# Four weight chunks to a group, and the low parts of the weights at another place in SBUF

## The chip, the cores and the metric

The kernel runs on one core of a Trainium2 chip. The metric is device time in microseconds (us): how long one execution takes. Matmuls run on TensorE (PE; PEld is its weight load), element-wise work on VectorE (DVE), ScalarE (ACT) and GpSimd (POOL), and the weights come by DMAs that SyncE (SP) issues.

## The reference

A two-layer decoder trunk over 256 tokens with 2048 features, all in float32. Layer 0 mixes tokens by a spatial gate beside a four-head attention into 256 memory tokens; layer 1 does it by a twelve-head latent attention beside the same memory attention. Each layer ends in a gated feed-forward network with a short convolution. Nearly all the work lies in the products with the weight matrices:

```python
D_MODEL, SEQ, D_FF = 2048, 256, 5632
def conv_ffn(h, w_up, cw, cb, w_down):
    a = h @ w_up                                   # 2048 x 11264
    ap = jnp.pad(a, ((0, 0), (CONV_W - 1, 0), (0, 0)))
    c = sum(ap[:, k:k + S] * cw[k] for k in range(CONV_W)) + cb
    gate, val = c[..., :D_FF], c[..., D_FF:]
    return (jax.nn.silu(gate) * val) @ w_down      # 5632 x 2048
...
for l in range(DEPTH):                             # DEPTH = 2
    ...
    x = x + jnp.concatenate([main, mo], axis=-1) @ w_out[l]
    x = x + conv_ffn(rmsnorm(x, g_ffn[l]), w_ffn_up[l], conv_w[l], conv_b[l], w_ffn_down[l])
return rmsnorm(x, g_final)
```

## The kernel before

**Three products for one.** The kernel multiplies in the type fp32r and cuts each operand in two: a high part, the copy in fp32r, and a low part, what that copy leaves of the float32 value. A product of weights W and activations X is then W_hi X_hi + W_hi X_lo + W_lo X_hi.

**Most products hold the weights still** (`gemm_fm` and `mm_fm`). An activation tile such as `xhl`, `h`, `mainhl`, `memhl`, `qhl` or `chl` has 512 columns for a block of 128 features: 256 high ones, then 256 low ones. For each 128x128 block of weights there is one **high product** (line L158): the block of `whi` is loaded into the array and all 512 columns stream past it; and one **low product** (L162): the block of `wlo` is loaded and only the 256 high columns stream. In the last layers the roles are turned round (`gemm_tm`, lines L213 to L215): blocks of activations are loaded, and `whi` and `wlo` stream; at the very end a few of these have only 256 columns.

**Chunks.** A weight chunk is 512 KB, 128 partitions by 1024 floats: two blocks of 128 rows by 512 columns, so 8 high and 8 low products. `chunk` takes a buffer `raw` (4 of them), issues the DMA into it on SP (L107), lets ACT round it into `whi` (4 buffers, L117; with a gain L122), and lets DVE write the rest, raw minus high, into `wlo` (4 buffers, L118; with a gain L123).

**Groups.** `gemm_fm` takes the chunks of a product two at a time (`together = 2`), so 16 high products stand in a row and then 16 low ones. Every second group is turned (low ones first), so that two runs of a kind meet: in the steady state 32 high, 32 low, 32 high and so on, the last run of a product and the first run of the next included. A product over 2048 features has 8 chunks, so four groups before. The very first product (`raw` is given) takes one chunk at a time, and `queries` and `keys` in layer 1 have groups of their own.

**Hooks.** Other work of the PE (transposes, attention scores and the like) is handed to `gemm_fm` as `hooks`, a table from the number of a chunk to functions. They are called after the group that holds the chunk. In layer 1 the last two heads go through the output projection `w_out` in this way: `turn` transposes their softmax (L970) and `attend` multiplies it with the values (L979, L980).

**Order.** A scheduler with its own estimates of times orders each engine's instructions, except in a few stretches that are written out by hand.

**Places.** In the built program `raw`, `whi`, `wlo` and all the activation tiles named above begin at byte 96 modulo 256 of a partition. `low_tile` gives `wlo` 64 spare floats; where it holds still, its data begin 16 floats further on, so at 160 modulo 256. Where `wlo` streams (`moves`), its data begin at 96. Every block in a tile begins at a multiple of 512 bytes from there.

Of the kernel before, what the change touches and what calls it, by code (L numbers as in the profile page):

```python
# [9 lines left out]
F32R = mybir.dt.float32r  # L10
# [6 lines left out]
P = 128  # L17
# [52 lines left out]
class Kernel:  # L70
# [20 lines left out]


    def low_tile(self, moves=False):
        w = self.wp.tile([P, 1088], F32R, tag="wlo", name=self.uid("wlo"), bufs=4)
        return w[:, :1024] if moves else w[:, 16 : 16 + 1024]


    def chunk(self, src, nk, ncol, gains=None, heads=None, raw=None, moves=False):
# [51 lines left out]

    def mm_fm(self, jobs, turn):
        mm = self.nc.tensor.matmul

        def high(js):
            for acc, wh, wl, x, first, last in js:
                mm(acc[:, :], wh, x, start=first, stop=last)  # L158

        def low(js):  # L160
            for acc, wh, wl, x, first, last in js:
                mm(acc[:, S:], wl, x[:, :S], start=False, stop=False)  # L162

        starts, ends = any(j[4] for j in jobs), any(j[5] for j in jobs)
        if ends and (starts or not turn):
            high([j for j in jobs if not j[5]])
            low(jobs)
            high([j for j in jobs if j[5]])
        elif turn and not starts:
            low(jobs)  # L170
            high(jobs)
        else:
            high(jobs)
            low(jobs)


    def gemm_fm(self, src, kbs, nblk, rhs, evict, nk=2, gain=None, hooks={}, raw=None):
        accs = [self.psum() for _ in range(nblk)]
        together = 1 if raw is not None else 2
        chunks = list(range(0, len(kbs), nk))  # L180
        groups = [chunks[i : i + together] for i in range(0, len(chunks), together)]

        def split(group):
            jobs = []
            for c in group:
                g = None if gain is None else [gain(kbs[c + i]) for i in range(nk)]
                hi, lo = self.chunk(src(kbs[c], nk), nk, nblk * P, g, raw=raw if c == 0 else None)
                for b in range(nblk):
                    cols = slice(b * P, (b + 1) * P)
                    for i in range(nk):  # L190
                        kk = c + i
                        jobs.append((accs[b], hi[:, i, cols], lo[:, i, cols], rhs(kbs[kk]), kk == 0, kk == len(kbs) - 1))
            return jobs

        ready = []
        for n, group in enumerate(groups):
            ahead = groups[n : n + 2] if raw is not None else [group]
            for g in ahead[len(ready) :]:
                ready.append(split(g))
                for f in hooks.get(-1, ()) if g is groups[0] else ():  # L200
                    f()
            self.mm_fm(ready.pop(0), n % 2 if raw is None else 0)
            for c in group:
                for f in hooks.get(c // nk, ()):
                    f()
        for b in range(nblk):
            evict(b, accs[b])

# [162 lines left out]
    def gain(self, name, k, n=1):  # L371
        c = self.g[name] + k
        return self.gT[:, c : c + n]
# [434 lines left out]
    def layer_b(self):  # L808
# [3 lines left out]
        w, wkv = t["w_in_b"][0], t["w_kv_a"]  # L812
# [5 lines left out]
        with tc.tile_pool(name="lb", bufs=1) as lb:  # L818
# [71 lines left out]
            hooks = {6: [rotate_key], 4: [lambda: fq(qhl, QR, "g_q_lat")]}  # L890
# [75 lines left out]
            def turn(h):  # L966
                p = pa.pop(h)
                acc = self.psum()
                for i in range(3):
                    nc.tensor.transpose(acc[:, i * P : (i + 1) * P], p[:, i * P : (i + 1) * P], self.ident)  # L970
                pT = self.tmp(lp, [P, 512], "pT", 3)
                nc.scalar.activation(pT[:, : 3 * P], acc[:, : 3 * P], AF.Copy)
                pa[h] = pT

            def attend(h):
                pT = pa.pop(h)
                o = self.psum()
                cols = slice(h * P, (h + 1) * P)
                mm(o[:, :S], v[:, 0, cols], pT[:, :S], start=True, stop=False)  # L979
                mm(o[:, P:S], v[:, 1, cols], pT[:, S : S + P], start=False, stop=True)  # L980
                self.split(hl[:, h, :], o[:, :S])
# [11 lines left out]
            n = GH // 2  # L993
# [27 lines left out]
            for h in (2 * n - 4, 2 * n - 3):  # L1021
                attend(h)
            ends = (2 * n - 2, 2 * n - 1)
            hooks = {2: [lambda h=h: turn(h) for h in ends], 3: [lambda h=h: attend(h) for h in ends]}
            self.w_out(1, hl, [12, 13, 14, 15] + list(range(12)), hooks, ctx.close)

    def run(self):
# [96 lines left out]
```

## Time and profile before

| What | Value |
|---|---|
| median of three runs | 2093.12 us (2093.07 to 2093.68) |
| the profiled execution | 2094.34 us, of which 2092.6 us are the span from the first to the last instruction |
| busy in the span | PE 2082.2 us, PEld 1821.7, DVE 1458.7, ACT 1139.0, POOL 398.9 |
| granted TensorE clock | 0.999 of full speed |
| read from HBM | 387.88 MB |

An entry "line engine op out<-in xcount | busy, mean" of the groups gives how many instructions of a kind there were and how long one took on average. Matmuls are pipelined, so their durations overlap; what a matmul adds to the time is the distance between two starts, which the timeline and the chain of waits give.

### The profile page before, as it was taken

How to read it: one execution, taken by the hardware profiler on the slowest of the kernel's cores; microseconds unless marked ns; L12 is line 12 of the kernel's file. 1: busy time of each engine (PE TensorE's matmuls, PEld its weight loads, DVE VectorE, ACT ScalarE, POOL GpSimd, SP SyncE). 2: the span in 40 equal slices, each digit the busy share in tenths (PEclk: the TensorE clock that was granted, in tenths of full speed). 3: DMA queues.
4: the chain of work that ended last, by engine and by line, in shares of the span. 5: the costliest groups of instructions: out<-in, count | busy, mean ns of one | idle time of the engine just before them, and what ended most of it. 6: DMA issues, size and time to landing. Idle time of an engine off the chain costs nothing.

```text
span 2092.6 us, 31012 instructions
## 1 busy us (share of the span) xinstructions
PE 2082.2 (100%) x11614; PEld 1821.7 (87%) x11614; DVE 1458.7 (70%) x2150; ACT 1139.0 (54%) x1747; POOL 398.9 (19%) x387
## 2 busy tenths in 40 slices
PE   9999999999999999999999999999999999999998
PEld 8888888888888888888888888888888888888886
DVE  6755767777756777567798875777765677746775
ACT  6754654555535655445655664456553565535554
POOL 0100133312101211012244121421210122201220
PEclk9999999999999999999999999999999999999999
DMA  8665555656556565556555534555655556555554
GB/s 272 197 216 159 161 195 188 191 188 195 191 192 191 181 201 188 194 185 190 190 192 182 176 106 159 185 190 181 192 194 194 186 188 194 196 196 189 184 191 152
DMA packets 208092, 392.01 MB, mean 187 GB/s; under 512 B 14334, under 2 KB 23876, under 8 KB 207812
## 3 DMA queue, kind: packets, MB, share of 16 engines
q1 hardware_dynamic: 207364, 388.98, 57.3%
q8 instruction: 91, 1.49, 0.3%
q10 hardware_dynamic: 576, 1.05, 0.2%
q14 instruction: 61, 0.50, 0.1%
HBM read 387.88 MB, written 2.10 MB: 186 GB/s over the span
## 4 chain that ended last, share of the span: by engine, by line
PE 99%; DMA 0%; ACT 0%; DVE 0%; issue 0%; ACTq 0%
PE ps L158 51%; PE ps L162 26%; PE ps L215 6%; PE ps L213 6%; PE ps L214 6%; PE ps L949 0%; PE ps L947 0%; PE ps L575 0%; PE ps L610 0%; DMA raw<-in_w_mem_kv 0%; PE ps L432 0%; PE ps L979 0%; PE ps L760 0%; PE ps L872 0%; PE ps L970 0%; PE ps L1051 0%
## 5 line engine op out<-in xcount | busy, mean ns | idle before, releaser
L118 DVE TENSOR_TENSOR wlo<-raw,whi 128x1024 fp32r<-128x1024 f32 x660 | 842.5, 1286 | 468.1 <-ACT whi L117 346.0
L117 ACT ACTIVATE whi<-raw 128x1024 fp32r<-128x1024 f32 x660 | 695.6, 1058 | 692.3 <-PE ps L158 511.3
L158 PE MATMUL ps<-xhl,whi 128*128 128x512 f32 x3264 | 765.0, 390 | 0.0
L158 PEld LDWEIGHTS ps<-xhl,whi 128*128 128x128 f32 x3264 | 605.1, 188 | 121.2
L662 POOL TENSOR_TENSOR a<-js,rbc 128x256 f32<-128x256 f32 x176 | 232.1, 1331 | 1094.1 <-DVE js L264 998.5
L162 PEld LDWEIGHTS ps<-xhl,wlo 128*128 128x128 f32 x3264 | 400.8, 189 | 8.4
L162 PE MATMUL ps<-xhl,wlo 128*128 128x256 f32 x3264 | 404.8, 281 | 0.0
L158 PE MATMUL ps<-h,whi 128*128 128x512 f32 x704 | 164.7, 390 | 0.0
L665 ACT ACTIVATE c<-a,cT 128x256 f32<-128x256 f32 x176 | 105.2, 598 | 98.6 <-POOL a L662 97.0
L158 PEld LDWEIGHTS ps<-h,whi 128*128 128x128 f32 x704 | 130.5, 188 | 26.0
L214 PE MATMUL ps<-wlo,h 128*128 128x512 f32 x354 | 137.1, 388 | 0.0
L213 PE MATMUL ps<-whi,h 128*128 128x512 f32 x354 | 137.0, 388 | 0.0
L215 PE MATMUL ps<-whi,h 128*128 128x512 f32 x354 | 136.6, 388 | 0.0
L158 PE MATMUL ps<-mainhl,whi 128*128 128x512 f32 x512 | 120.1, 390 | 0.0
L158 PEld LDWEIGHTS ps<-mainhl,whi 128*128 128x128 f32 x512 | 94.8, 188 | 18.9
L667 DVE SCALAR_TENSOR_TENSOR c<-a,cT,c 128x254 f32<-128x254 f32 x176 | 101.0, 586 | 0.0
L666 DVE SCALAR_TENSOR_TENSOR c<-a,cT,c 128x255 f32<-128x255 f32 x176 | 91.7, 540 | 12.9 <-ACT c L665 12.7
L123 DVE SCALAR_TENSOR_TENSOR wlo<-raw,gT,whi 128x512 fp32r<-128x512 f32 x112 | 87.1, 819 | 19.3 <-ACT whi L122 17.5
L122 ACT ACTIVATE whi<-raw,gT 128x512 fp32r<-128x512 f32 x112 | 74.7, 723 | 31.6 <-PE ps L158 14.2
L264 DVE TENSOR_TENSOR js<-ps,cr 128x256 f32<-128x256 f32 x209 | 82.2, 415 | 12.4 <-POOL a L662 12.4
L262 ACT ACTIVATE cr<-ps 128x256 f32<-128x256 f32 x243 | 79.7, 374 | 15.7 <-PE ps L158 12.1
L162 PEld LDWEIGHTS ps<-h,wlo 128*128 128x128 f32 x704 | 86.5, 189 | 1.9
(259 smaller groups left out, 1859.6 us busy)
## 6 DMA issues: line engine op xcount, KB each, us to landing
raw<-in_w_ffn_up SPq DMA_DIRECT2D x352, 512.0 KB, 3.5
raw<-in_w_ffn_down SPq DMA_DIRECT2D x176, 512.0 KB, 4.3
raw<-in_w_out SPq DMA_DIRECT2D x64, 512.0 KB, 3.5
raw<-in_w_in_a SPq DMA_DIRECT2D x56, 512.0 KB, 4.0
raw<-in_w_mem_kv SPq DMA_DIRECT2D x31, 512.0 KB, 3.8
raw<-in_w_in_b SPq DMA_DIRECT2D x16, 512.0 KB, 3.5
raw<-in_w_kv_a SPq DMA_DIRECT2D x9, 512.0 KB, 4.2
raw<-in_w_uq SPq DMA_DIRECT2D x12, 384.0 KB, 3.3
```

The source lines that it names most:

```text
L117: nc.scalar.activation(hi[:, :n], raw[:, :n], AF.Copy)
L118: nc.vector.tensor_tensor(lo[:, :n], raw[:, :n], hi[:, :n].bitcast(F32), ALU.subtract)
L123: nc.vector.scalar_tensor_tensor(lo[:, s], raw[:, s], gains[k], hi[:, s].bitcast(F32), ALU.mult, ALU.subtract)
L158: mm(acc[:, :], wh, x, start=first, stop=last)
L162: mm(acc[:, S:], wl, x[:, :S], start=False, stop=False)
L213: mm(acc, xh, wh, start=first, stop=False)
L214: mm(acc, xh, wl, start=False, stop=False)
L215: mm(acc, xl, wh, start=False, stop=last)
L662: nc.gpsimd.tensor_tensor(a, self.join(acc), rb, ALU.mult)
L665: nc.scalar.activation(c, a, AF.Identity, scale=w(2), bias=w(3))
L666: nc.vector.scalar_tensor_tensor(c[:, 1:], a[:, : S - 1], w(1), c[:, 1:], ALU.mult, ALU.add)
L667: nc.vector.scalar_tensor_tensor(c[:, 2:], a[:, : S - 2], w(0), c[:, 2:], ALU.mult, ALU.add)
```

## The change

- `gemm_fm` takes four chunks together (one, as before, in the first product). A product of 8 chunks has two groups: 32 high, 32 low, and then 32 low, 32 high; with the neighbours that makes runs of 64.
- `wlo` has six buffers instead of four. `raw` and `whi` keep four.
- `mm_fm` gets a function `between`, called between the two kinds of a group. `gemm_fm` hands it the hooks of the first half of the group's chunks; those of the second half follow the group. One hook in layer 1 gets another number (2 becomes 1).
- The data of a still `wlo` begin 19 floats on instead of 16: at 172 modulo 256 instead of 160. The activation tiles move up by 2 x 4352 bytes, which leaves them at 96 modulo 256.

```diff
     def low_tile(self, moves=False):
-        w = self.wp.tile([P, 1088], F32R, tag="wlo", name=self.uid("wlo"), bufs=4)
-        return w[:, :1024] if moves else w[:, 16 : 16 + 1024]
+        w = self.wp.tile([P, 1088], F32R, tag="wlo", name=self.uid("wlo"), bufs=6)
+        return w[:, :1024] if moves else w[:, 19 : 19 + 1024]
...
-    def mm_fm(self, jobs, turn):
+    def mm_fm(self, jobs, turn, between=lambda: None):
...
         if ends and (starts or not turn):
             high([j for j in jobs if not j[5]])
+            between()
             low(jobs)
             high([j for j in jobs if j[5]])
         elif turn and not starts:
             low(jobs)
+            between()
             high(jobs)
         else:
             high(jobs)
+            between()
             low(jobs)
...
-        together = 1 if raw is not None else 2
+        together = 1 if raw is not None else 4
...
-            self.mm_fm(ready.pop(0), n % 2 if raw is None else 0)
-            for c in group:
-                for f in hooks.get(c // nk, ()):
-                    f()
+
+            def hooked(cs):
+                for c in cs:
+                    for f in hooks.get(c // nk, ()):
+                        f()
+
+            self.mm_fm(ready.pop(0), n % 2 if raw is None else 0, lambda: hooked(group[: len(group) // 2]))
+            hooked(group[len(group) // 2 :])
...
-            hooks = {2: [lambda h=h: turn(h) for h in ends], 3: [lambda h=h: attend(h) for h in ends]}
+            hooks = {1: [lambda h=h: turn(h) for h in ends], 3: [lambda h=h: attend(h) for h in ends]}
```

What this does to the built order is shown at two places. The first is on PE, at the end of the first product of layer 1's output projection: `ps_12738` to `ps_12741` are its four sums, `ps_12969` to `ps_12972` those of the next product, `mainhl` the activations. Before:

```order
L162 MATMUL ps_12740<-mainhl_11640,wlo_12898 128x256 x2
L162 MATMUL ps_12741<-mainhl_11640,wlo_12898 128x256 x2
L158 MATMUL ps_12969<-mainhl_11640,whi_12974 128x512
L162 MATMUL ps_12738<-mainhl_11640,wlo_12904 128x256
L162 MATMUL ps_12739<-mainhl_11640,wlo_12904 128x256
L162 MATMUL ps_12740<-mainhl_11640,wlo_12904 128x256
L162 MATMUL ps_12741<-mainhl_11640,wlo_12904 128x256
L158 MATMUL ps_12969<-mainhl_11640,whi_12974 128x512
L158 MATMUL ps_12970<-mainhl_11640,whi_12974 128x512
L162 MATMUL ps_12738<-mainhl_11640,wlo_12904 128x256
```

After, at the same place:

```order
L162 MATMUL ps_12740<-mainhl_11640,wlo_12872 128x256 x2
L162 MATMUL ps_12741<-mainhl_11640,wlo_12872 128x256 x2
L158 MATMUL ps_12738<-mainhl_11640,whi_12853 128x512 x2
L158 MATMUL ps_12739<-mainhl_11640,whi_12853 128x512 x2
L158 MATMUL ps_12740<-mainhl_11640,whi_12853 128x512 x2
```

The high products of the next product no longer stand between the low ones. Over the whole program a high product follows a low one directly at 170 places before and at 92 after; a low one follows a high one at 176 and at 99.

The second is on DVE, in the feed-forward network of layer 0, where one product has just ended and its sums `ps_7356` to `ps_7359` go through the convolution (`js`, `c`, `hv`) while the low parts of the next weights are written. Before:

```order
L118 TENSOR_TENSOR wlo_7643<-raw_7641,whi_7642 128x1024
L264 TENSOR_TENSOR js_7539<-ps_7356,cr_7537 128x256
L264 TENSOR_TENSOR js_7553<-ps_7357,cr_7551 128x256
L118 TENSOR_TENSOR wlo_7649<-raw_7647,whi_7648 128x1024
L264 TENSOR_TENSOR js_7567<-ps_7358,cr_7565 128x256
L264 TENSOR_TENSOR js_7581<-ps_7359,cr_7579 128x256
L666 SCALAR_TENSOR_TENSOR c_7542<-a_7536,cT,c_7542 128x255
L666 SCALAR_TENSOR_TENSOR c_7556<-a_7550,cT,c_7556 128x255
L667 SCALAR_TENSOR_TENSOR c_7542<-a_7536,cT,c_7542 128x254
L118 TENSOR_TENSOR wlo_7687<-raw_7685,whi_7686 128x1024
```

After:

```order
L118 TENSOR_TENSOR wlo_7611<-raw_7609,whi_7610 128x1024
L271 TENSOR_TENSOR js_7539<-ps_7356,cr_7537 128x256
L271 TENSOR_TENSOR js_7553<-ps_7357,cr_7551 128x256
L118 TENSOR_TENSOR wlo_7617<-raw_7615,whi_7616 128x1024
L271 TENSOR_TENSOR js_7567<-ps_7358,cr_7565 128x256
L271 TENSOR_TENSOR js_7581<-ps_7359,cr_7579 128x256
L118 TENSOR_TENSOR wlo_7687<-raw_7685,whi_7686 128x1024
L673 SCALAR_TENSOR_TENSOR c_7542<-a_7536,cT,c_7542 128x255
L673 SCALAR_TENSOR_TENSOR c_7556<-a_7550,cT,c_7556 128x255
L674 SCALAR_TENSOR_TENSOR c_7542<-a_7536,cT,c_7542 128x254
L118 TENSOR_TENSOR wlo_7693<-raw_7691,whi_7692 128x1024
```

The low part of the fifth chunk (`wlo_7687`), which stood behind three of the convolution's steps on `c`, now stands ahead of them; otherwise the mixture is much the same. `wlo_7611` and `wlo_7617` now belong to the third and fourth chunk of the same first group.

## The prediction

> **What bounds the kernel.** First the page's busy times, then PE's waits, then the shares of the chain that ended last.
>
> ```profile
> span 2092.6 us, 31012 instructions
> ...
> PE 2082.2 (100%) x11614; PEld 1821.7 (87%) x11614; DVE 1458.7 (70%) x2150; ACT 1139.0 (54%) x1747; POOL 398.9 (19%) x387
> ...
> PEclk9999999999999999999999999999999999999999
> ...
> PE 99%; DMA 0%; ACT 0%; DVE 0%; issue 0%; ACTq 0%
> PE ps L158 51%; PE ps L162 26%; PE ps L215 6%; PE ps L213 6%; PE ps L214 6%; PE ps L949 0%; PE ps L947 0%; PE ps L575 0%; PE ps L610 0%; DMA raw<-in_w_mem_kv 0%; PE ps L432 0%; PE ps L979 0%; PE ps L760 0%; PE ps L872 0%; PE ps L970 0%; PE ps L1051 0%
> ```
>
> ```profile
> PE ps L513 <- DVE ones L312: 1.1, 1, 1.1
> PE ps L356 <- DMA graw<-in_g_mem: 0.3, 1, 0.3
> PE ps L979 <- ACT pT L972: 0.3, 1, 0.3
> PE ps L158 <- DVE memhl L482: 0.2, 1, 0.2
> ```
>
> PE is the chain: 99% of the span, at full granted clock, and it waits 1.9 us in all. High products (L158) carry 51%, low ones (L162) 26%. There is no wait worth removing. Only two things can shorten the span: less distance between two products, or fewer disturbances where the kinds change. So I need the distances. The chain in order of time, inside a feed-forward product, gives the start of each run, its length in us, and its count:
>
> ```profile
> 1001.98 7.28 PE ps L158 x32
> 1009.25 3.77 PE ps L162 x32
> 1013.02 7.28 PE ps L158 x32
> ```
>
> A low product takes 3.77/32 = 117.8 ns, a high one 227.5 ns on average. For the steady pace of 512 columns I take the end of the kernel, where the weights stream and nothing changes kind; two rows of the chain, 13 rounds of three products apart:
>
> ```profile
> 2047.83 0.23 PE ps L215
> ...
> 2056.67 0.23 PE ps L215
> ```
>
> 8.84 us over 39 products is 226.7 ns. The last few products there have 256 columns (timeline, start first):
>
> ```profile
> 2082.69 0.28 PE L214 MATMUL ps<-wlo,h 128*128 128x256 f32 x1
> ...
> 2083.89 0.28 PE L215 MATMUL ps<-whi,h 128*128 128x256 f32 x1
> ```
>
> Ten products in 1.20 us: 120.0 ns. So 256 columns more cost 106.7 ns, and each product pays 226.7 - 213.3 = 120.0 - 106.7 = 13.3 ns on top of its columns. In these products the loaded block stands at 96 modulo 256 bytes. Low products of the steady state have theirs at 160, and pay 117.8 - 106.7 = 11.1 ns. What remains to be gained in a low product is this 11.1 ns. The surcharge isn't fixed even at 160, as two other places show. One is in layer 1's output projection, behind an interruption by other matmuls; the other is the rotary key (L872), the only product in which low parts at 160 meet 512 columns:
>
> ```profile
> 1281.80 1.98 PE L162 MATMUL ps<-mainhl,wlo 128*128 128x256 f32 x16
> 1283.62 0.40 PE L158 MATMUL ps<-mainhl,whi 128*128 128x512 f32 x1
> ```
>
> ```profile
> 1139.00 1.97 PE L872 MATMUL ps<-xhl,whi 128*128 128x512 f32 x8
> 1140.82 2.03 PE L872 MATMUL ps<-xhl,wlo 128*128 128x512 f32 x8
> 1142.68 1.55 PE L158 MATMUL ps<-xhl,whi 128*128 128x512 f32 x6
> ```
>
> The 16 low products take 1.82 us, 113.8 ns each: a surcharge of 7.1 ns with the same tiles, places and shapes as in the steady run. The eight of L872 with `wlo` take 232.5 ns where the eight with `whi` take 227.5, so here 160 is worse than 96. The surcharge depends on how the load of a block falls against the columns streaming past, and the place of the block is one of the things that set it.
>
> **The change, part by part.** The sum is made against the profiled execution: 2094.34 us, of which 2092.6 are the span; it is 1.2 us above the median 2093.12, from which I subtract.
>
> *Place of the low parts.* It bears on every low product. The groups of PE count them:
>
> ```profile
> L162 PE MATMUL ps<-xhl,wlo 128*128 128x256 f32 x3264 | 404.8, 281 | 0.0
> L162 PE MATMUL ps<-h,wlo 128*128 128x256 f32 x704 | 87.0, 281 | 0.0
> L162 PE MATMUL ps<-mainhl,wlo 128*128 128x256 f32 x512 | 63.4, 281 | 0.0
> L162 PE MATMUL ps<-memhl,wlo 128*128 128x256 f32 x128 | 17.6, 283 | 0.1
> L162 PE MATMUL ps<-qhl,wlo 128*128 128x256 f32 x72 | 9.7, 280 | 0.0
> L162 PE MATMUL ps<-chl,wlo 128*128 128x256 f32 x48 | 7.0, 282 | 0.0
> ```
>
> 4728 products, all on the path, so 1 ns is 4.7 us. No product of this trace loads a block at 172. Bounds: no surcharge at all gives 4728 x 11.1 ns = 52 us less; the surcharge of L872 (232.5 - 213.3 = 19.2 ns) gives 4728 x 8.1 = 38 us more. The nearest rows are those at 160, twelve bytes off, with two paces, 117.8 and 113.8. I take 113.8: the faster pace, once an interruption has brought it about, holds through the run, so both are patterns that keep themselves up, and a block that begins three floats off need not fall into the slower one. That is a judgement between two rows and the weakest step here. It gives 4728 x 4.0 = 19 us less.
>
> [...]
>
> *Runs of 64.* What a change of kind costs is seen in the durations behind it: the first five high products of a run, and 25 later ones of the same run (groups in two narrow windows):
>
> ```profile
> L158 PE MATMUL ps<-xhl,whi 128*128 128x512 f32 x5 | 1.3, 393 | 0.0
> ```
>
> ```profile
> L158 PE MATMUL ps<-xhl,whi 128*128 128x512 f32 x25 | 5.8, 389 | 0.0
> ```
>
> 5 x 4 ns = 20 ns for each change from low to high, and 7.28 - 32 x 0.2267 = 0.026 us says the same. The built order has 92 such changes instead of 170: 78 x 20 ns = 1.6 us less. Bounds: nothing, if the 20 ns are paid later, and 2.0 us by the second figure.
>
> *Groups of four: when the data are due.* This is the step that could add a wait. Rows for what must be done in time:
>
> ```profile
> L118 DVE TENSOR_TENSOR wlo<-raw,whi 128x1024 fp32r<-128x1024 f32 x660 | 842.5, 1286 | 468.1 <-ACT whi L117 346.0
> L117 ACT ACTIVATE whi<-raw 128x1024 fp32r<-128x1024 f32 x660 | 695.6, 1058 | 692.3 <-PE ps L158 511.3
> ...
> L662 POOL TENSOR_TENSOR a<-js,rbc 128x256 f32<-128x256 f32 x176 | 232.1, 1331 | 1094.1 <-DVE js L264 998.5
> ...
> raw<-in_w_ffn_up SPq DMA_DIRECT2D x352, 512.0 KB, 3.5
> ```
>
> ```profile
> ACT whi L117 <- PE ps L158: 511.3, 340, 6.9
> DVE wlo L118 <- PE ps L162: 106.1, 62, 2.3
> ```
>
> Both splits mostly wait for PE to free a buffer: they run ahead. After the change the tightest place is the second group's last chunk. Its `whi` buffer is freed when the first group's high products end; ACT 1.06 and DVE 1.29 make it ready 2.4 us later. Its low products begin 32 + 24 low products later, 56 x 0.118 = 6.6 us. With six `wlo` buffers its low buffer is freed after 16 low products, at 1.9 us; with DVE's 1.29 that is 3.2 us. The cover is 3.4 us, and what may eat it is the work on the product before, on DVE in the same row: its four steps through POOL are 4 x 1.33 = 5.3 us long, start at the product's end and are over before the 7.28 us of the first high run are. So I cost it at nothing, with 0 and 4 us as ends. DMAs: in a high run of 64, eight chunks are used in 14.6 us, 287 GB/s against 190 over a period of 22.1 us; four `raw` and four `whi` buffers are filled in the 7.5 us of low products, and a chunk lands in 3.5 us. Nothing.
>
> *Hooks.* The same instructions at places that differ by a few us; PE's only hook wait is the 0.3 us on `pT` (L979). `turn` now comes after 32 high products, 7.3 us into the product, `attend` 3.8 us later: nothing, up to 0.5 us.
>
> *DVE and ACT* write the same bytes; DVE's write to 172 instead of 160 lies beside PE, with DVE idle for 30% of the span. Nothing.
>
> Sum: -19 - 1.6 + 1 (about a quarter of the 4.5 us to which the upper ends of groups and hooks add up) = -19.6 us, so 2093.1 - 19.6 = 2073.5 us.
>
> **Rivals.** *The place does nothing.* Then only the switches count: 2093.1 - 1.6 = 2091.5. For it: 96 and 160 differ by 2.2 ns in low products only. Against: they differ, and in both directions. [...]
>
> [...]
>
> *PE waits for the low parts.* Were each of the about 72 products with several groups to wait 0.3 us, that is 22 us, and the gain of the place is gone: 2095. Against it: the cover of 3.4 us.
>
> *The place is much better.* With the surcharge halved again, to 3.6 ns, the pace is 110.3: 4728 x 7.5 = 35 less, 2056. Nothing in the trace shows such a pace.
>
> **How the numbers follow.** The main case 0.40 (its own range 2065 to 2083, half way to the paces 110.3 and 117.8 beside it), much better 0.11, nothing 0.21, worse 0.22, waits 0.06. A change of under 0.2% (4.2 us) is what a measurement can't tell from none. Faster: the first two, 0.51. Same: "nothing" and half of "waits", 0.24. Slower: "worse" and the other half, 0.25. The range 2052 to 2104 leaves out a part of "much better" and half of "worse", some 0.15.
>
> **What would show it.** A low run of 64 in the chain lasting 7.25 us (113.3 to 113.8 ns each) proves the place; 7.54 us, no effect; over 7.6, the rival. High runs of 64 should begin with about five products of 393 ns and go on at 389, once in 64. PE's waits should stay under 6 us in all, with none on `wlo`; a row "PE ps L162 <- DVE wlo L118" with tens of us would be the third rival. Should the high pace leave 226.7 ns, my account of the surcharge is wrong.

## The result, and the profile after

The changed kernel takes 2077.98 us (median of four runs, 2077.57 to 2078.2) against 2093.11 (2093.07 to 2093.68) for the kernel before: a ratio of 0.9927, 95% interval 0.991 to 0.9944, or 15.1 us less. Predicted were 2073.5. The profiled execution took 2078.11 us, 2076.4 of them span; its page, in the parts that were shown of before:

```profile
span 2076.4 us, 30990 instructions
...
PE 2062.8 (99%) x11614; PEld 1802.2 (87%) x11614; DVE 1461.1 (70%) x2150; ACT 1133.3 (55%) x1747; POOL 386.3 (19%) x387
...
PEclk9999999999999999999999999999999999999999
...
PE 97%; POOL 1%; DVE 1%; ACT 0%; issue 0%; DMA 0%; POOLq 0%; ACTq 0%
...
L118 DVE TENSOR_TENSOR wlo<-raw,whi 128x1024 fp32r<-128x1024 f32 x660 | 833.2, 1270 | 486.2 <-ACT whi L117 460.2
L117 ACT ACTIVATE whi<-raw 128x1024 fp32r<-128x1024 f32 x660 | 697.8, 1059 | 621.4 <-PE ps L158 413.8
```

The same 11,614 matmuls at the same clock; PE is busy for 19.4 us less. Now 2% of the chain that ended last lies on POOL and DVE, where there was none: a first hint of new waits. The chain in order of time, in a feed-forward product (start, length, what):

```profile
990.17 14.53 PE ps L158 x64
1004.70 7.27 PE ps L162 x64
1011.97 14.53 PE ps L158 x64
```

Low products come every 7.27/64 = 113.6 ns where they came every 117.8, high ones every 227.0 where it was 227.5. Low products show it in the groups too:

```profile
L162 PE MATMUL ps<-xhl,wlo 128*128 128x256 f32 x3264 | 382.0, 277 | 0.0
...
L162 PE MATMUL ps<-h,wlo 128*128 128x256 f32 x704 | 83.7, 277 | 1.6 <-ACT h L276 1.3
```

277 ns is how long a product lasts, against 281 before, and there is an idle time of 1.6 us that wasn't there, 1.3 of it behind ACT's `h`. PE's waits in all, in the form "who waited, for what: us in total, times, longest":

```profile
PE ps L162 <- ACT h L276: 1.3, 2, 0.7
PE ps L301 <- POOL ssum L311: 1.1, 2, 0.6
PE ps L520 <- DVE ones L319: 1.1, 1, 1.1
PE ps L158 <- DVE memhl L489: 0.3, 1, 0.3
PE ps L986 <- ACT pT L979: 0.3, 1, 0.3
```

The first two are new. None is on `wlo`, which was the one that I had worked out.

For exact sums I added the distances from each matmul's start to the next one's, by line, over the whole program. High products (L158) take 1080.7 us before and 1078.8 after; low ones (L162) 558.7 and 543.6. With -1.9 and -15.1 these two lines carry the result; the three lines of the last layers stay at 366 us together.

### The profile page after: what moved, and what is told of

It is laid out like the page before. It is cut to its first block, busy times and chain, and to the rows that moved or that the text cites. A ratio compares the mean times of both kernels' runs of the same rounds, so it can differ in the third digit from the quotient of the medians.

```text
span 2076.4 us, 30990 instructions
## 1 busy us (share of the span) xinstructions
PE 2062.8 (99%) x11614; PEld 1802.2 (87%) x11614; DVE 1461.1 (70%) x2150; ACT 1133.3 (55%) x1747; POOL 386.3 (19%) x387
## 4 chain that ended last, share of the span: by engine, by line
PE 97%; POOL 1%; DVE 1%; ACT 0%; issue 0%; DMA 0%; POOLq 0%; ACTq 0%
PE ps L158 50%; PE ps L162 25%; PE ps L221 6%; PE ps L220 6%; PE ps L222 6%; POOL ssum L311 0%; POOL sq L310 0%; PE ps L956 0%; DVE wlo L118 0%; POOL a L669 0%; PE ps L954 0%; PE ps L582 0%; PE ps L617 0%; PE ps L439 0%; PE ps L986 0%
## 5 line engine op out<-in xcount | busy, mean ns | idle before, releaser
L118 DVE TENSOR_TENSOR wlo<-raw,whi 128x1024 fp32r<-128x1024 f32 x660 | 833.2, 1270 | 486.2 <-ACT whi L117 460.2
L158 PE MATMUL ps<-xhl,whi 128*128 128x512 f32 x3264 | 754.6, 390 | 0.0
L158 PEld LDWEIGHTS ps<-xhl,whi 128*128 128x128 f32 x3264 | 608.4, 188 | 124.1
L669 POOL TENSOR_TENSOR a<-js,rbc 128x256 f32<-128x256 f32 x176 | 210.5, 1208 | 1103.6 <-DVE js L271 962.3
L162 PEld LDWEIGHTS ps<-xhl,wlo 128*128 128x128 f32 x3264 | 379.8, 188 | 4.3
L162 PE MATMUL ps<-xhl,wlo 128*128 128x256 f32 x3264 | 382.0, 277 | 0.0
L158 PE MATMUL ps<-h,whi 128*128 128x512 f32 x704 | 163.0, 390 | 0.0
L158 PEld LDWEIGHTS ps<-h,whi 128*128 128x128 f32 x704 | 131.1, 188 | 26.6
L158 PE MATMUL ps<-mainhl,whi 128*128 128x512 f32 x512 | 118.0, 390 | 0.0
L158 PEld LDWEIGHTS ps<-mainhl,whi 128*128 128x128 f32 x512 | 95.5, 188 | 19.5
L673 DVE SCALAR_TENSOR_TENSOR c<-a,cT,c 128x255 f32<-128x255 f32 x176 | 93.8, 552 | 10.6 <-ACT c L672 9.4
L162 PEld LDWEIGHTS ps<-h,wlo 128*128 128x128 f32 x704 | 82.7, 188 | 3.6 <-ACT h L276 2.4
L162 PE MATMUL ps<-h,wlo 128*128 128x256 f32 x704 | 83.7, 277 | 1.6 <-ACT h L276 1.3
```

The lines of the kernel that those rows point to most:

```text
L118: nc.vector.tensor_tensor(lo[:, :n], raw[:, :n], hi[:, :n].bitcast(F32), ALU.subtract)
L669: nc.gpsimd.tensor_tensor(a, self.join(acc), rb, ALU.mult)
L673: nc.vector.scalar_tensor_tensor(c[:, 1:], a[:, : S - 1], w(1), c[:, 1:], ALU.mult, ALU.add)
```

## The experiments

Two theories stood after the result. The first: the place of `wlo` does it, and the rest of the change is worth a microsecond or two either way. The second: longer runs and fewer changes do it, or the place only in runs of 64.

**The place alone.** The kernel before with one number changed.

```diff
-        return w[:, :1024] if moves else w[:, 16 : 16 + 1024]
+        return w[:, :1024] if moves else w[:, 19 : 19 + 1024]
```

> The kernel before with the place alone changed: low parts at 172 modulo 256, groups of two, four buffers for low parts. Theory 1 (the place sets the pace of the low products): from the fourth product of a low run on, 113.3 ns between starts as in the changed kernel; 3.65 us for a run of 32 instead of 3.77; with about 29 of 32 products gaining 4.45 ns, 4728 x 0.91 x 4.45 = 19 us less, 2074 us, and none of the changed kernel's new waits (the sum ssum behind POOL, h behind ACT), so about 4 us below the changed kernel. Theory 2 (the long runs bring the faster pace, the place nothing): 117.8 ns and 2093 us.

Measured: 2076.45 us (2076.38 to 2076.45) beside 2093.53, ratio 0.992 (0.9906 to 0.9933). The chain:

```profile
988.42 3.64 PE ps L162 x32
992.07 7.28 PE ps L158 x32
```

A low run of 32 takes 3.64 us instead of 3.77; high runs are as before. The place alone brings the whole gain and 1.5 us more than the full change. A time some 4 us below the changed kernel's was expected: low products do take 3.0 us less than there (540.6 against 543.6), but high ones take 2.1 more (1080.9 against 1078.8).

**Everything but the place.** The changed kernel with the old number.

```diff
-        return w[:, :1024] if moves else w[:, 19 : 19 + 1024]
+        return w[:, :1024] if moves else w[:, 16 : 16 + 1024]
```

> The changed kernel with the place alone undone: low parts at 160, groups of four, six buffers. Theory 1: 117.8 ns in runs of 64, 7.54 us each; the switches' gain of 1.9 us and the new waits' loss of some 4.5 us are left, so 2095 to 2097 us, slower than before. Theory 2: 113.3 ns and 2078 us.

Measured: 2095.99 us (2094.92 to 2096.69), ratio 1.0012 (1.0003 to 1.0021).

```profile
992.74 7.54 PE ps L162 x64
1000.28 14.53 PE ps L158 x64
```

7.54/64 = 117.8 ns: runs of 64 alone don't bring the faster pace. Groups of four cost some 2.5 us, although high products take 1.8 us less than before (1078.9 against 1080.7). The new waits are here as well:

```profile
PE ps L301 <- POOL ssum L311: 1.0, 2, 0.5
PE ps L162 <- ACT h L276: 0.9, 2, 0.4
```

**The next step of four bytes: 176.** The changed kernel with one float more.

```diff
-        return w[:, :1024] if moves else w[:, 19 : 19 + 1024]
+        return w[:, :1024] if moves else w[:, 20 : 20 + 1024]
```

> The changed kernel with the low parts 20 floats on, at 176 modulo 256, which is a multiple of 16 bytes again. Read from the trace: pace of the low products. Theory 1a (what helps is leaving the 16-byte step, since 160 and 96 are both on it): 117.8 to 120 ns, 2095 us or more. Theory 1b (what matters is the distance from the streaming columns' place, 172 and 176 being nearly the same): 113 to 114 ns, about 2078 us.

Measured, one run: 2102.24 us.

```profile
995.33 7.59 PE ps L162 x64
```

118.6 ns. A block that begins one float later is slower than at 160. That is what the theory of the 16-byte step foretold; the sweep below shows that the step has no such meaning.

**The high parts at 172 too.** `whi` gets spare floats like `wlo`.

```diff
+    def high_tile(self, moves=False):
+        w = self.wp.tile([P, 1088], F32R, tag="whi", name=self.uid("whi"), bufs=4)
+        return w[:, :1024] if moves else w[:, 19 : 19 + 1024]
...
-        hi = self.wp.tile([P, 1024], F32R, tag="whi", name=self.uid("whi"), bufs=4)
+        hi = self.high_tile(moves)
```

> The changed kernel with the still high parts at 172 as well (the whi tiles made 64 floats longer, their data 19 floats on where they hold still). If a block at 172 is better against any stream: high products under 226.7 ns, by up to the low products' 4.45 ns, then up to 4728 x 4.45 = 21 us less, 2057 us. If it is as with L872, where blocks at 160 did worse than at 96 against 512 columns (232.5 against 227.5 ns): 231 to 234 ns, 20 to 31 us more, 2098 to 2109 us.

Measured, one run: 2106.41 us. In this kernel L162 is the line of the high products and L166 that of the low ones:

```profile
1004.85 14.93 PE ps L162 x64
1019.78 7.29 PE ps L166 x64
```

The place that speeds up 256 columns slows down 512: 233.3 ns a product instead of 227.0. Low products keep their 113.3 in the steady state beside it.

**All 64 places of the low parts.** Each of 64 products of the output projections and the feed-forward networks takes another place for its `wlo`: 96 + 4 j modulo 256 for the j-th.

```diff
+        if gain is None and nk == 2:
+            mine = self.turns % 64 if self.turns >= 0 else 19
+            self.turns += 1
...
-        return w[:, :1024] if moves else w[:, 19 : 19 + 1024]
+        return w[:, :1024] if moves else w[:, self.off : self.off + 1024]
```

> The changed kernel, but each of 64 products (the 8 of the output projections, the 44 and 12 of the feed-forward networks) has its low parts at another place: 96 + 4 j modulo 256 for the j-th. Read from the trace: the pace of the low products at each place, with 117.8 at 160, 113.3 at 172 and 118.6 at 176 as known points. Theory 1a (leaving the 16-byte step helps): the sixteen multiples of 16 at 117 to 120, all others lower. Theory 1b (the distance to the streaming columns decides, in some larger step): a pattern that repeats every 32, 64 or 128 bytes and doesn't follow the 16-byte step. Total anywhere from 2080 to 2105 us.

Measured, one run: 2097.17 us. In this kernel L159 is the line of the high products and L163 that of the low ones. Four places in a row, in the chain; the low runs are those at 172, 176, 180 and 184:

```profile
703.56 7.27 PE ps L163 x64
710.83 14.54 PE ps L159 x64
725.37 7.59 PE ps L163 x64
732.96 14.56 PE ps L159 x64
747.52 7.68 PE ps L163 x64
755.21 14.53 PE ps L159 x64
769.74 7.28 PE ps L163 x64
```

And the slowest, place 44:

```profile
1653.25 7.88 PE ps L163 x64
```

The steady pace at each place is the mean distance between starts, from the ninth product of a run on (mostly 55 values each, without the distances that a wait makes longer). The first column is the place of the row's first entry; entries are four bytes apart, in ns:

```text
  0  119.9 117.7 120.0 118.8 118.1 113.3 117.7 118.4
 32  117.8 118.4 120.0 123.3 116.7 117.3 120.0 120.6
 64  116.6 120.1 118.4 119.9 117.3 119.9 117.7 119.9
 96  120.0 118.3 115.5 116.6 118.2 120.0 121.9 116.7
128  118.4 120.0 119.2 117.8 118.4 120.1 117.8 119.5
160  117.8 118.3 118.4 113.3 118.7 120.0 113.3 118.3
192  117.4 120.0 117.7 120.0 120.0 118.9 119.4 118.7
224  120.1 118.7 118.0 120.0 120.0 116.6 117.3 120.0
```

Three places reach 113.3: 20, 172 and 184. 43 of the 64 lie above the 117.8 of place 160. An entry is one product, mostly a single run, and a place can have more than one pace, as 160 has; so the table tells what a run at a place did, and not the best that the place can do. Place 172 has more behind it: all 59 runs of 64 in the changed kernel, and all 126 runs of 32 or more in the kernel with the place alone, go at 113.3 outside the waits. Whether a place is a multiple of 16 bytes isn't what sets this: the sixteen multiples go from 116.6 to 120.1 and none is among the three best.

**All 64 places of the high parts.** The same with `whi`, while `wlo` stays at 172; `mine` counts as in the other sweep.

```diff
+    def high_tile(self, moves=False):
+        w = self.wp.tile([P, 1088], F32R, tag="whi", name=self.uid("whi"), bufs=4)
+        return w[:, :1024] if moves else w[:, self.off : self.off + 1024]
```

> The changed kernel, but each of the same 64 products has its still high parts at another place, 96 + 4 j modulo 256; the low parts stay at 172. Read: the pace of the high products at each place, with 226.7 at 96 and 233.3 at 172 as known points. If 96 is the best for 512 columns: nothing under 226.7. If some places do for 512 columns what 172 does for 256: 222 to 224 ns there. Total 2085 to 2105 us.

Measured, one run: 2098.01 us. Five places run at 226.7: 80, 92, 96, 216 and 228. The others take 228.3 to 237.8 on average, many of them 230.0 or 233.3. 96, which both kernels use, is one of the best already.

Here, too, one place can have two paces. The high products of one place come in two runs of mostly 32: the first stands directly behind high products at the place before, the second behind low ones. At 44, 84, 240 and 252 the first run goes at 226.7, and the second at 235.9, 233.3, 233.6 and 238.0. In the chain (L163 is the high line here) the first row is 32 products at 80 and then 32 at 84, the second 32 at 84 and then 32 at 88:

```profile
1948.56 14.53 PE ps L163 x64
1970.36 14.91 PE ps L163 x64
```

**Place, or distance?** Two kernels tell whether what counts is the byte at which a block begins, or how far it lies from something else. First, eight unused floats ahead of everything move every tile by 32 bytes:

```diff
+        self.pad = cp.tile([P, 8], F32, name="pad")
+        nc.vector.memset(self.pad, 0.0)
         self.ident = cp.tile([P, P], F32, name="ident")
```

> The changed kernel with eight unused floats per partition ahead of everything else, so that every tile moves up by 32 bytes: whi, xhl and the rest to 128, the still low block to 204 modulo 256; the distance between them stays as it was. Theory 1, that the pace of products goes by the places relative to one another: low 113.3 ns, high 226.7 ns, about 2078 us. Theory 2, that it goes by the absolute place of the weight block as the two sweeps show it: low 120.0 (place 204), 4728 x 6.7 ns = +32 us, high 233.3 (place 128), about 4766 x 6.6 ns = +31 us, about 2140 us. Between: one of the two paces moves alone, about 2109 us.

Measured, one run: 2079.04 us, high and low blocks at 128 and 204.

```profile
991.71 14.53 PE ps L158 x64
1006.24 7.27 PE ps L162 x64
```

Nothing moved, though in the sweeps these two places had 233.3 and 120.0. So it is a distance. Then 32 unused floats ahead of the activation tiles alone:

```diff
+        self.apad = self.ap.tile([P, 32], F32, name="apad")
+        self.nc.vector.memset(self.apad, 0.0)
         self.x = self.ap.tile([P, NB, S], F32, name="xT")
```

> The changed kernel with 32 unused floats per partition ahead of the activation tiles alone: xhl, h, mainhl and the others move from 96 to 224 modulo 256, while raw and whi stay at 96 and wlo at 172. Theory 1, that the pace goes by the distance from the streamed tile to the loaded block: a low block then lies 52 bytes below the tile that streams, where the sweep had 123.3 ns (place 44), 4728 x 10 ns = +47 us; a high block lies 128 off, where the sweep of high places had 232.9, 4728 x 6.2 ns = +29 us; and the last layers' products, whose roles are turned round, are 128 off too, up to 1600 x 6 ns = +10 us. Sum about 2155 to 2165 us. Theory 2, that it goes by the distance between the weight tiles themselves (wlo against whi or raw): no change, about 2078 us.

Measured, one run: 2144.35 us.

```profile
992.26 7.89 PE ps L162 x64
1000.15 14.88 PE ps L158 x64
1015.03 7.67 PE ps L162 x64
```

High products come every 232.5 ns, low ones every 123.3 in the first run and 119.8 in the second; over all 59 low runs of 64, waits included, a run takes 7.78 us, 121.6 a product. By line: high +24.3 us, low +33.0, the last layers +8.7 over the changed kernel, together the 66 us. Nothing of the weights was moved; so the distance to the tile that streams counts. The low part is smaller than the 47 us that I had taken from the one run at place 44: in the steady state 29 of the 59 runs go at 123.3, 28 at 120.0 and two at 113.3. What decides between the three at this distance isn't shown. Last, with the same move, the still blocks follow the activations to 224 and 44, while `raw` stays (`high_tile` as above, and for `wlo`):

```diff
-        return w[:, :1024] if moves else w[:, 19 : 19 + 1024]
+        return w[:, :1024] if moves else w[:, 51 : 51 + 1024]
...
+        return w[:, :1024] if moves else w[:, 32 : 32 + 1024]
```

> The same move of the activation tiles by 128 bytes, but the blocks of the products with still weights follow them: whi's data begin 32 floats on (at 224) and wlo's 51 floats on (at 44), while raw stays at 96. Theory 1: low 113.3 and high 226.7 ns again in the products with still weights; only the last layers' products, whose weights stream from 96, are 128 bytes off and may lose up to 10 us, so 2078 to 2088 us. If raw or anything else that stays in place has a part in it, low or high stays off those paces.

Measured, one run: 2087.98 us; L162 is the high line here.

```profile
992.57 14.53 PE ps L162 x64
1007.10 7.27 PE ps L166 x64
```

Both paces are back (high 1078.8 us, low 543.7, to 0.1 us those of the changed kernel). What is left, 10 us, are the last layers, whose weights still stream from 96 past blocks at 224: 376.0 us against 366.3. So the pace of a product goes by the distance, modulo 256 bytes, between the block that is loaded and the tile that streams, together with what stands ahead of its run. Fast were 76 bytes up (in every run), 88 up and 76 down (one run each) for 256 columns; 0 (in 72 runs of 76; the others 227.1), 4 or 16 down and 120 or 132 up (two runs each) for 512. That 256 is the period, and not 512, is seen inside the runs: the buffers of `wlo` are 4352 bytes long, 17 times 256, and from the second chunk of a run on all chunks go at 113.3 or 113.4. Half of it isn't a period: 172 had 113.3 and 44 had 123.3.

**An interruption at place 160.** The basis of my price was that 160 has two paces, and that an interruption leads to the faster.

```diff
+                if raw is None and n % 2 == 0 and len(group) == 4:
+                    spare = self.psum()
+                    self.nc.tensor.matmul(spare[:, :P], self.ones, self.ones, start=True, stop=True)
```

> The changed kernel with its low block at 160 again (2096 us, low products 117.8 ns) and one more product of 128 x 128 on constant data between the high and the low run of nearly every full group of four, some 70 in all; its result is not used. The prediction took its price from rows in which low products at 160 ran at 113.3 after an interruption. If an interruption brings the faster pace about and it then holds: the runs of 64 behind such a product go at 113.3, up to 59 x 64 x 4.5 ns = 17 us less, the added products cost about 70 x 0.15 = 10 us, so 2086 to 2092 us and L162's mean falls. If the pace belongs to the place alone: 117.8 stays in all runs and the time is 2104 to 2110 us.

Measured, one run: 2097.64 us. The chain at the same place as above:

```profile
992.72 0.22 PE ps L215 x2
992.94 7.26 PE ps L162 x64
1000.21 14.54 PE ps L158 x64
```

The same tiles, places and shapes now take 7.26 us instead of 7.54. Of 72 added products 63 stand ahead of low ones, and behind 60 of those the low run goes on at 113.3 to its end or to its next wait: behind all 56 that follow a high run, and behind four of the seven that follow something else. In the other three it stays at 117.8. So the mechanism is as expected, and the time isn't: low products take 11.4 us less (550.3 against 561.7), but an added product takes 142 ns and the first low one behind it 201 instead of 118, so that the 72 cost 10.2 us on their own line; the high line takes 1.3 more. That comes to +0.1 us; the span is 1.0 us longer than with 160 alone (2095.9 against 2094.9), and the rest isn't explained.

**Without the two new waits.** The timeline of PE shows the wait on `h` in the changed kernel: at the first product of a down projection over 16 blocks, PE gets to the low products of the last blocks too early.

```profile
544.04 6.52 PE L162 MATMUL ps<-h,wlo 128*128 128x256 f32 x56
551.24 1.59 PE L162 MATMUL ps<-h,wlo 128*128 128x256 f32 x8 [0.67 <-ACT h L276]
```

The other is the sum of squares for the norm (`ssum`, a group of a narrow window at the start of layer 0's feed-forward network):

```profile
L301 PE MATMUL ps<-ssum,ones 128*128 128x256 f32 x2 | 0.7, 431 | 0.6 <-POOL ssum L311 0.6
```

The edit moves that hook to a later chunk, and takes two chunks at a time where `h` is new.

```diff
-        first = {1: [lambda: self.rstd_bc(rb, ssum, D)]}
+        first = {5: [lambda: self.rstd_bc(rb, ssum, D)]}
...
-        together = 1 if raw is not None else 4
+        together = 1 if raw is not None else most
...
+                    self.gemm_fm(..., most=2 if j == 0 and ng == 4 else 4)
```

> The changed kernel with its two new waits taken away: in the feed-forward network the sum over the features (rstd_bc) is called in the fifth chunk's place instead of the second's, behind all low products; and the first down product of a part with 16 blocks keeps groups of two, so that the low products of its last chunk begin some 3.6 us later. If these waits are what the groups of four give back: PE's waits on ssum and on h gone, some 4 us less than the changed kernel, 2074 us, and 2.5 us below groups of two at 172 (g2_p172, 2076.45). If the groups cost something else as well: 2076 to 2078 us.

Measured: 2073.63 us (2073.09 to 2074.19), ratio 0.9905 (0.9888 to 0.9921). PE's waits:

```profile
PE ps L520 <- DVE ones L319: 1.1, 1, 1.1
PE ps L439 <- DMA mtok<-in_mem: 0.4, 2, 0.2
PE ps L986 <- ACT pT L979: 0.3, 1, 0.3
PE ps L363 <- DMA graw<-in_g_mem: 0.2, 1, 0.2
```

Both waits are gone, low products take 539.0 us, and the time is 4.4 us below the changed kernel's. It beats both kernels.

## Why the prediction was right, and where it was off

*Place of the low parts: right in sign and size, by a ground that holds only in part.* The pace taken was 113.8 ns; measured are 113.3 in the steady state, so 4728 x 4.5 = 21 us less instead of 19. The claim that the two paces at 160 are patterns that keep themselves up is shown by the kernel with the interruption (60 of 63 runs). The step from there to 172, that a block three floats off "need not fall into the slower one", was no ground: at 176, 180 and 168 the pace is 118.7, 120.0 and 118.4, and in the sweep only 3 of 64 places had what I forecast. From the trace of before alone the chance of 0.40 was too high; that 172 is one of the three was not to be read there, so that this term came out right was luck.

*L872.* Its 232.5 ns for `wlo` at 160 spoke for a worse place, to which I gave 0.22. But it streams 512 columns, and widths have tables of their own: in the sweep of high places 160 has 233.2 ns and 172 has 233.3, while low products go at 113.3 at 172, and at 117.8 at 160.

*The bound "no surcharge at all", 106.7 ns,* took the surcharge of 13.3 ns as the same for both widths. The lowest paces found are 226.7 and 113.3, so the narrow product gets by with 6.6 over the same columns; nothing came below that in 64 places, and the rival "much better" has no place here.

*Runs of 64: right.* High products take 1.9 us less against 1.6. The runs begin as forecast, five products and then 24 later ones of the same run (groups in two narrow windows):

```profile
L158 PE MATMUL ps<-xhl,whi 128*128 128x512 f32 x5 | 1.3, 394 | 0.0
```

```profile
L158 PE MATMUL ps<-xhl,whi 128*128 128x512 f32 x24 | 5.6, 389 | 0.0
```

Low runs have such a beginning too, which I left out: in a run of 64 the first three products come every 117.5 to 118.4 ns before the pace settles, 14 ns a run. It is a part of the difference below.

*Groups of four: when the data are due. This is the step that failed.* "So I cost it at nothing": I worked the cover out for `wlo`, and there it held; no wait on `wlo` came. What I didn't work out are the other data whose use the new order brings forward. The low products of blocks 14 and 15 of `h` now come after 32 high and 56 or 60 low ones, 7.25 + 56 x 0.1134 = 13.6 and 14.1 us into the product; by groups of two they came after 48 high and as many low ones, 10.9 + 56 x 0.1178 = 17.5 and 18.0. ACT finished these blocks 12.6 and 14.4 us into the product before, and 14.4 and 15.3 after. A slack of 3.5 us and more became a wait of 0.8 us at two places; with three longer distances behind it (0.2 to 0.4 us instead of 0.11) this takes 2.7 us by the distances. A part of it is ACT's own, which came 1.8 and some 0.9 us later than before: at its old times block 14 would have been ready (12.6 against 13.6) and block 15 late by 0.3 us. The hook on `ssum` is the same kind: PE now gets there 9.1 us into the product and POOL has the sum at 9.8; before, PE got there at 10.6. With the few slower products behind it this takes 1.9 us at its two places. The kernel without the two waits prices it: 4.4 us on the median, where I had allowed 1 for groups and hooks together.

*Hooks.* "Nothing, up to 0.5 us" holds for `turn` and `attend`: the wait on `pT` is 0.3 us, as before. I didn't look at the one hook that bears on the feed-forward networks.

*DVE and ACT: right.* DVE 1461.1 us busy against 1458.7, and PE waits for neither split.

The sum by its own terms, for low products: 4728 x 4.5 = -21.3, beginnings of runs +1.6 (539.0 - 4728 x 0.1133 = 3.3 without the waits, against 558.7 - 4728 x 0.1178 = 1.7 before), waits +4.6 (543.6 - 539.0): -15.1. With the switches' -1.9 it is -17.0; the span lost 16.2.

*The rival "the place does nothing"* is the kernel that keeps 160: it gave 2095.99, not 2091.5, in good part because of the same waits (1.0 us on `ssum`, 0.9 on `h`, and the slower products behind them).

With an equal number of products on equal data the distance between the loaded block and the tile that streams moves the time from 2077.98 us to 2144.35. What in the chip makes it so isn't shown; the runs show only that the distance modulo 256 and what stands ahead of a run count.

## What to carry to other kernels

Where PE is the bound and every product loads a new block, measure the pace of the steady state for several distances between the loaded block and the tile that streams, each width by itself; 4 ns of 118 were worth 0.8% here, and a wrong distance cost more (66 us) than a right one brought (17). Such a place is found by a sweep in one run, one product after the other, and not by reasoning from one neighbour (168 and 176 had 118.4 and 118.7 ns beside the 113.3 of 172); as one distance can have several paces, the best ones need more than one run each before they are trusted; after that every tile that is moved has to keep the distance. And when an order is changed, work out for every operand of the moved products when it is due, the ones that another engine makes just before included, not only for the buffers that the change is about.

## What of the hardware was unexpected

- The pace of back-to-back products with a new block each depends on the distance between block and streamed tile modulo 256 bytes: 113.3 to 123.3 ns for 256 columns, there with neighbours four bytes apart up to 6.7 ns from one another, and 226.7 to 237.8 for 512. I saw no simple rule in the two sweeps.
- At the same distance two paces can hold, 117.8 and 113.3 ns at 64 bytes and 256 columns; one other product of 142 ns ahead of a low run brought the faster one, to the run's end or to its next wait, in 60 of 63 runs. At 52 bytes down there were three: 113.3, 120.0 and 123.3.
- Moving all tiles together by 32 bytes moved neither pace (2079.04 us).
